# Layer 0 starts its first three projection chunks on rows that carry the scale only, and adds the shift's share as one column per chunk

## The chip, the cores and the metric

The kernel runs on one core of a Trainium2 chip. The metric is the device time of one launch in microseconds (us), as the median of several runs. The engines of the core are named as in the profile: PE is TensorE (PEld its weight loads), DVE is VectorE, ACT is ScalarE, POOL is GpSimd, and SP is the engine whose queue issues the DMAs. L379 is line 379 of the kernel before.

## The reference, cut to what matters

Two decoder layers work on 1024 tokens of width 1024. Each sub-layer computes `x + gate(c) * RMSNorm(f(RMSNorm(x) * (1 + scale(c)) + shift(c)))`. `scale`, `shift` and `gate` are columns of one modulation `silu(c) @ ada_w + ada_b`, the same for all tokens. In layer 0, f starts with one input projection of the modulated rows, `h @ w_in`, whose columns are: a small group (the position part of the keys and the 16 step sizes dt), the latents, 1536 channels xbc, and 1024 channels z. The xbc channels pass through a causal convolution of width 4, a SiLU and the state-space scan.

With a = g * (1 + scale), n the normalised row and s the shift, the row is h = n * a + s, and so h @ w = (n * a) @ w + s @ w. The second term is one number for each output channel, the same for all tokens.

## The kernel before, in words

All rows of the projection's input lie transposed in SBUF (`hT`): two halves of 512 tokens, each with 8 blocks k of 128 of the 1024 inputs, and each block as a pair hi, lo. hi is the value rounded to the type of the matmul, lo is the rest. A chunk is 128 output channels. For one half of a chunk PE runs 24 matmuls of 128x512: for each k hi by hi, hi by lo and lo by hi (L113 to L115, in `mm3`, called from `dense_t`). The weights of a chunk are loaded as one block of 512 KB and split into hi (ACT, L131) and lo (DVE, L132). `chunk` runs both halves and empties the PSUM bank of each (`each`), and then calls `after`.

`first_h` makes `hT` for layer 0. The modulation columns j=1 (scale) and j=0 (shift) are each built from eight 512 KB blocks of `ada_w`: DVE multiplies each by silu(c) and accumulates (L366, L368), and `ada_cols` sums over the partitions on PE (L283, 8 matmuls with a column of ones, recorded as 16). `normal(i)` loads a tile of 128 tokens, ACT takes its sum of squares (L157), POOL makes 1/rms (L150, L151), ACT (i below 4, L350) or DVE (L388) scales the rows, PE transposes 8 blocks (L357) and ACT copies them out (L358) into `xT`. Only when scale and shift are both there, DVE makes v = xT * a + s (L379), ACT writes hi (L143) and DVE or POOL in turn writes lo (L144), for 8 blocks of each half. Tiles 0 to 3 are the first half, tiles 4 to 7 the second.

`mixer0_ssd` then runs the chunks: first three side by side (misc, xbc 0, xbc 1), each first half and then each second half, then xbc 2 to 11 one by one, then z 0 and z 1, then the other z chunks and two latent chunks merged with the state-space scan (`ssd_scan`). `misc` feeds `dt_chain`, a chain of small steps over PE, DVE and ACT (L556 to L579), whose result `csT` goes to DRAM and is read back repeated over the partitions (`csb`, L694, and `esb`, L700). `after` of an xbc chunk is the convolution: four DVE passes over 1024 tokens (L621, L623), a tanh on ACT (L544), one more DVE pass (L545) and the store to DRAM (L549), from where the scan reads it back (L680, L689).

`split_w` and `pump` also push one step of a background job at each weight load: the other modulation columns (`ada_later`, L255, L271, L273).

No order is written out by hand here. A planner lays out the queue of every engine at build time, by the order of the program, by what its own model says is ready and by free buffers. So an engine's order in the trace differs from the order of the source. SP issues all loads and stores of this stage in one queue.

Of the kernel before, what the change touches and what calls it, by code (L numbers as in the profile page):

```python
# [21 lines left out]
P = 128  # L22
T = 1024
NT = T // P
D = 1024
# [21 lines left out]
class Trunk:  # L47
# [292 lines left out]

    def first_h(self, pool, hT):

        nc, I = self.nc, self.I
        xT = self.t(pool, [P, KD, T], "xT")

        def normal(i):
            xt = self.t(pool, [P, D], "xt", bufs=4)
            nc.sync.dma_start(xt, self.x[i])
            if i < 4:
                nc.scalar.activation(xt, xt, AF.Copy, scale=self.rstd(self.sumsq(xt), 1, 1.0 / D))  # L350
            else:
                self.normalise(xt, xt)
            for q in range(2):
                ps = self.bk()
# [3 lines left out]
                nc.scalar.copy(xT[:, 4 * q:4 * q + 4, i * P:(i + 1) * P], ps.rearrange("p (k c) -> p k c", c=P))  # L358

        for j in (1, 0):  # L360
            acc = self.t(pool, [P, 1024], f"acc{j}")
            for i in range(KD):
                w = self.t(pool, [P, 1024], "aw", bufs=5)
                nc.sync.dma_start(w, I["l0_ada_w"][i * P:(i + 1) * P, j * 1024:(j + 1) * 1024])
                if i == 0:
                    nc.vector.tensor_scalar(acc, w, self.cs[:, 0:1], None, op0=ALU.mult)  # L366
                else:
                    nc.vector.scalar_tensor_tensor(acc, w, self.cs[:, i:i + 1], acc, op0=ALU.mult, op1=ALU.add)  # L368
                if i in (1, 4):
                    normal(2 * (1 - j) + i // 4)  # L370
            if j == 1:
                self.setup_gains()
                a = self.ada_scale(0, 1, self.ada_cols(acc), self.gains[0, "mix"])
        self.w0 = self.split_w(self.ring, I["l0_w_in"][0])
        s = self.ada_shift(0, 0, self.ada_cols(acc))
        for h, hs in enumerate(HALVES):
            for k in range(KD):
                v = xT[:, k, hs]
                nc.vector.tensor_scalar(v, v, a[:, k:k + 1], s[:, k:k + 1], op0=ALU.mult, op1=ALU.add)  # L379
                al = slice(0, 512)  # L380
                self.split(self.hk(hT, h, 0, k, al), self.hk(hT, h, 1, k, al), v, nc.gpsimd if k % 2 else nc.vector)
            if h == 0:
                for i in range(4, NT):
                    normal(i)

# [194 lines left out]

    def mixer0_ssd(self, hT, keep):

# [6 lines left out]
        with ExitStack() as e:  # L589
            tmp = self.pool(e, "mix0")  # L590
            sp = self.pool(e, "ssd")
            S["dsk"] = self.t(tmp, [P, 8], "dsk")
# [13 lines left out]
            def misc(h, hs, ps):  # L606
                nc.scalar.copy(mi[0:64, hs], ps[0:64, :])
                nc.vector.tensor_copy(dtT[:, hs], ps[64:80, :])

# [3 lines left out]

            def xbc(j, **kw):
# [11 lines left out]
                return self.chunk("l0_w_in", 6 + j, hT,  # L626
                                  lambda h, hs, ps: nc.scalar.copy(v[:, 3 + h * 512:3 + (h + 1) * 512], ps), after, **kw)

# [22 lines left out]

            self.side_by_side(self.chunk("l0_w_in", 0, hT, misc, misc_end, w=self.w0), xbc(0), xbc(1, bank=self.cx))
            for j in range(2, XBC_N):
                self.side_by_side(xbc(j))

# [1450 lines left out]
    def layer0(self, ew):  # L2106

        self.scratch()
        with ExitStack() as e0:
            self.h_pools(e0, "right")  # L2110
            hT = [self.hT_blocks(4 * h) for h in range(2)]
            with ExitStack() as e:
                self.first_h(self.pool(e, "pre"), hT)
            self.bg = [self.ada_later(0, 2, "gate_m0"), self.ada_later(0, 3, "sf0"), self.ada_later(0, 4, "af0")]
            ek = ExitStack()
            self.mixer0_ssd(hT, self.pool(ek, "keep0"))
            self.mixer0_latent(hT, self.pool(ek, "keepq"))
            self.drain()
# [160 lines left out]
```

## Time and profile before

| what | value |
|---|---|
| median of 3 runs | 3250.03 us (3245.92 to 3252.7) |
| the profiled execution's own time | 3248.5 us |
| its span in the trace | 3246.5 us |
| PE busy in the span | 3038.8 us (94%) |
| DVE, ACT, POOL busy | 2146.6 us (66%), 1310.1 us (40%), 712.9 us (22%) |
| 16 DMA engines, mean | 156 GB/s over the span |
| granted clock of PE, mean | 0.972 |

PE's busy time covers nearly the whole span, so idle stretches of PE are the places where the span can become shorter. The page's picture in 40 slices shows PE at 5 tenths in the first slice (81 us) and at 7 to 9 tenths in slices 3 to 6.

### The profile page before, as it was taken

How to read it: one execution, taken by the hardware profiler on the slowest of the kernel's cores; microseconds unless marked ns; L12 is line 12 of the kernel's file. 1: busy time of each engine (PE TensorE's matmuls, PEld its weight loads, DVE VectorE, ACT ScalarE, POOL GpSimd, SP SyncE). 2: the span in 40 equal slices, each digit the busy share in tenths (PEclk: the TensorE clock that was granted, in tenths of full speed). 3: DMA queues.
4: the chain of work that ended last, by engine and by line, in shares of the span. 5: the costliest groups of instructions: out<-in, count | busy, mean ns of one | idle time of the engine just before them, and what ended most of it. 6: DMA issues, size and time to landing. Idle time of an engine off the chain costs nothing. (4 is left out here: it accounts for less than half of the span.)

```text
span 3246.5 us, 42945 instructions
## 1 busy us (share of the span) xinstructions
PE 3038.8 (94%) x15828; PEld 2462.2 (76%) x15828; DVE 2146.6 (66%) x3371; ACT 1310.1 (40%) x2159; POOL 712.9 (22%) x678
## 2 busy tenths in 40 slices
PE   5987799999999999999899998989999999999998
PEld 4776677777777788787788887777777777888787
DVE  6664366676888778667645546467766788678655
ACT  4343424454542223344533323345655542223443
POOL 3001224310104333001123124012322113322001
PEclk9998889999999999999999999999999999999999
DMA  6555534322655455887324435331211655455854
GB/s 215 138 152 155 145 109 140 101 91 65 225 170 189 156 194 191 288 298 237 116 104 130 137 100 153 89 127 58 80 40 53 237 172 192 156 210 192 293 197 161
DMA packets 246738, 508.00 MB, mean 156 GB/s; under 512 B 27872, under 2 KB 90144, under 8 KB 245504
## 3 DMA queue, kind: packets, MB, share of 16 engines
q1 hardware_dynamic: 246528, 505.26, 47.5%
q8 instruction: 125, 2.05, 0.3%
q14 instruction: 85, 0.70, 0.1%
HBM read 369.04 MB, written 136.13 MB: 156 GB/s over the span
## 5 line engine op out<-in xcount | busy, mean ns | idle before, releaser
L114 PE MATMUL bk<-slab,whi 128*128 128x512 f32 x1208 | 481.8, 399 | 1.9 <-DVE slab L144 1.9
L113 PE MATMUL bk<-slab,whi 128*128 128x512 f32 x784 | 326.0, 416 | 8.2 <-ACT ca L636 4.6
L115 PE MATMUL bk<-slab,wlo 128*128 128x512 f32 x784 | 314.1, 401 | 0.0
L114 PEld LDWEIGHTS bk<-slab,whi 128*128 128x128 f32 x1208 | 232.1, 192 | 53.5 <-issue 2.9
L113 PE MATMUL bk<-T,whi 128*128 128x512 f32 x528 | 210.2, 398 | 1.3 <-DVE blk L1378 1.3
L115 PE MATMUL bk<-T,wlo 128*128 128x512 f32 x528 | 207.9, 394 | 0.0
L113 PEld LDWEIGHTS bk<-slab,whi 128*128 128x128 f32 x784 | 153.1, 195 | 45.3 <-issue 5.4
L150 POOL TENSOR_SCALAR rstd<-ss 128x1 f32<-128x1 f32 (+1 forms) x86 | 32.4, 376 | 688.4 <-ACT junk L157 642.8
L115 PEld LDWEIGHTS bk<-slab,wlo 128*128 128x128 f32 x784 | 152.1, 194 | 33.5 <-issue 0.2
L1174 ACT ACTIVATE whi<-rawa 128x512 fp32r<-128x512 f32 (+1 forms) x108 | 80.6, 750 | 192.5 <-PE bk L114 162.7
L113 PE MATMUL cx<-slab,whi 128*128 128x512 f32 x368 | 146.3, 398 | 6.9 <-ACT blk L1226 5.2
L2095 POOL TENSOR_SCALAR pexp<-pexp,rs 128x640 f32<-128x640 f32 (+7 forms) x128 | 94.4, 741 | 243.8 <-DVE rs L2094 78.9
L114 PE MATMUL cx<-slab,whi 128*128 128x512 f32 x368 | 145.5, 395 | 0.9 <-DVE slab L144 0.9
L115 PE MATMUL cx<-slab,wlo 128*128 128x512 f32 x368 | 145.5, 395 | 0.0
L960 PE MATMUL sm<-ident,pexp 128*128 128x128 f32 x816 | 132.2, 278 | 5.2 <-DVE pexp L950 1.9
L273 DVE SCALAR_TENSOR_TENSOR adaacc<-ada,silu_c,adaacc 128x1024 f32<-128x1024 f32 x70 | 101.7, 1454 | 49.4 <-DMA ada<-in_l_ada_w_dram 49.4
L1402 POOL TENSOR_TENSOR blk<-blk,blk 128x512 f32<-128x512 f32 x22 | 35.3, 1603 | 422.0 <-DVE blk L1398 325.8
L960 PEld LDWEIGHTS sm<-ident,pexp 128*128 128x128 f32 x816 | 93.9, 140 | 40.5 <-issue 18.4
L1175 DVE TENSOR_TENSOR wlo<-rawa,whi 128x512 fp32r<-128x512 f32 (+1 forms) x108 | 118.5, 1097 | 7.4 <-ACT whi L1174 6.7
L113 PEld LDWEIGHTS bk<-T,whi 128*128 128x128 f32 x528 | 99.2, 188 | 26.8 <-DVE blk L1378 1.7
L2091 ACT ACTIVATE pexp<-pexp,nm 128x640 f32<-128x640 f32 (+7 forms) x128 | 94.0, 735 | 62.1 <-DVE nm L2089 49.6
L962 ACT COPY pT<-sm 128x512 f32<-128x512 f32 (+2 forms) x144 | 76.3, 530 | 104.8 <-PE sm L960 104.0
(623 smaller groups left out, 8517.6 us busy)
## 6 DMA issues: line engine op xcount, KB each, us to landing
ada<-in_l_ada_w_dram SPq DMA_DIRECT2D x80, 512.0 KB, 4.2
hid<-blk SPq DMA_DIRECT2D x154, 256.0 KB, 2.0
raw<-in_l_w_in_dram SPq DMA_DIRECT2D x51, 512.0 KB, 4.4
ab<-hid SPq DMA_DIRECT2D x96, 256.0 KB, 3.9
cat<-cat SPq DMA_DIRECT2D x64, 256.0 KB, 2.7
ab<-wt SPq DMA_DIRECT2D x60, 256.0 KB, 4.0
raw<-in_l_w_gate_dram SPq DMA_DIRECT2D x28, 512.0 KB, 3.9
raw<-in_l_w_up_dram SPq DMA_DIRECT2D x28, 512.0 KB, 4.5
```

Source lines behind the costliest of these rows:

```text
L113: mm(out, lh, rh, start=start, stop=False, skip_group_check=more)
L114: mm(out, lh, rl, start=False, stop=False, skip_group_check=more)
L115: mm(out, ll, rh, start=False, stop=stop, skip_group_check=more)
L150: nc.gpsimd.tensor_scalar(r, ss, inv_d, EPS, op0=ALU.mult, op1=ALU.add)
L273: ins = nc.vector.scalar_tensor_tensor(acc, raw, self.cs[:, k:k + 1], acc, op0=ALU.mult, op1=ALU.add)
L960: nc.tensor.transpose(ps[:, k * P:(k + 1) * P], e[:, (b + k) * P:(b + k + 1) * P], self.ident)
L962: (nc.scalar.copy if self.evac else nc.vector.tensor_copy)(pt[:, b:b + m, :], ps[:, :m * P].rearrange("p (k c) -> p k c", c=P))
L1174: nc.scalar.activation(hi, src, AF.Copy)
L1175: (eng or nc.vector).tensor_tensor(lo, src, hi.bitcast(F32), op=ALU.subtract)
L1402: ptt(c, c, state[pm, 0]["u3"], op=ALU.mult)
L2091: nc.scalar.activation(e, e, AF.Exp, bias=nm, scale=-1.0, accum_out=rs)
L2095: nc.gpsimd.tensor_scalar(e, e, rs, 0.0, op0=ALU.mult, op1=ALU.add)
```

## The change: what it does

The order of the first stage becomes: all blocks of the scale column (j=1) and tiles 0 to 3 interleaved; then the first weights; then the scale `a`. `scaled(h)` writes hi and lo of n * a, without the shift (ACT: hi with `a` as scale; DVE: one two-operand instruction for lo). The three first chunks (misc, xbc 0, xbc 1) run on these rows, half by half, into six PSUM banks that stay full. Tiles 4 to 7 are normalised between the first three half-chunks, and the shift column (j=0) is accumulated beside them. When s is there, 24 matmuls of one column (8 for each of the 3 chunks, on the unsplit weights) make s @ w, which is copied to `col`. `misc` and `xbc` add `col` when they empty their banks. Then `shifted(h)` makes the full rows in place: v = xT * a + s, hi on ACT, lo on DVE for three of four blocks and on POOL for the fourth. From xbc 2 on everything works on full rows; xbc 2 and 3 run side by side, and the rest one by one.

Buffers: `xT`, now in two halves, and the three raw weights lie in a pool of their own on the other side of SBUF, closed after the first three chunks' `after`; the scan's pool `sp` is opened behind that. The transposes use the two `sm` banks and no longer the four `bk` banks. The three first weights are split by `split_w` inside `first_h`, which does not push the background job.

```diff
@@ first_h
+        def scaled(h):
             for k in range(KD):
-                v = xT[:, k, hs]
+                v, c = xT[h][:, k, :], a[:, k:k + 1]
+                hi, lo = (self.hk(hT, h, p, k, al) for p in range(2))
+                nc.scalar.activation(hi, v, AF.Copy, scale=c)
+                nc.vector.scalar_tensor_tensor(lo, v, c, hi.bitcast(F32), op0=ALU.mult, op1=ALU.subtract)
+
+        def shifted(h):
+            for k in range(KD):
+                v = xT[h][:, k, :]
                 nc.vector.tensor_scalar(v, v, a[:, k:k + 1], s[:, k:k + 1], op0=ALU.mult, op1=ALU.add)
-                self.split(self.hk(hT, h, 0, k, al), self.hk(hT, h, 1, k, al), v, nc.gpsimd if k % 2 else nc.vector)
+                self.split(self.hk(hT, h, 0, k, al), self.hk(hT, h, 1, k, al), v, nc.gpsimd if k % 4 == 3 else nc.vector)
...
+        for i in range(4):
+            load_a(1, i)
+            load_x(i)
+        load_a(1, 4)
+        self.setup_gains()
+        for i in range(KD):
+            step(1, i)
+            if i + 5 < KD:
+                load_a(1, i + 5)
+            if i % 2:
+                normal(i // 2)
+        for n in range(2):
+            load_w(n)
+        load_x(4)
+        load_x(5)
+        a = self.ada_scale(0, 1, self.ada_cols(acc[1]), self.gains[0, "mix"])
...
+        split_w(0)
+        scaled(0)
+        dense(0, 0)
+        split_w(1)
+        normal(4)
+        normal(5)
+        dense(1, 0)
+        split_w(2)
+        normal(6)
+        normal(7)
+        dense(2, 0)
+        for i in range(KD):
+            step(0, i)
+            if i + 5 < KD:
+                load_a(0, i + 5)
+            if i == 3:
+                scaled(1)
+        dense(0, 1)
+        s = self.ada_shift(0, 0, self.ada_cols(acc[0]))
+        dense(1, 1)
+        ps = self.sm()
+        for n in range(3):
+            for k in range(KD):
+                nc.tensor.matmul(ps[:, n:n + 1], raws[n][:, k * P:(k + 1) * P], s[:, k:k + 1], start=(k == 0),
+                                 stop=(k == KD - 1))
+        col = self.t(self.small, [P, 3], "col", bufs=1)
+        nc.vector.tensor_copy(col, ps[:, :3])
+        dense(2, 1)
+        return banks, col, shifted
@@ mixer0_ssd
+            banks, col, shifted = first
+            three = [(misc, misc_end), xbc(0), xbc(1)]
+            for h, hs in enumerate(HALVES):
+                for (each, _), ps in zip(three, banks):
+                    each(h, hs, ps[h])
+                shifted(h)
+            for _, after in three:
+                after()
+            close_first.close()
+            sp = self.pool(e, "ssd")
+            two = [self.chunk("l0_w_in", 6 + j, hT, *xbc(j)) for j in (2, 3)]
+            self.side_by_side(*two)
```

## Rows read from the trace of the kernel before

**Rows 1.** Busy time of each engine by stretch, from the span's start: the stretch, its length, then PE, PEld, DVE, ACT and POOL busy in us (with their instructions), the granted clock of PE, the share of the DMA engines and what they moved.

```profile
0.00:10.00 10.00, 0.00 (x0) 0.00 (x0) 2.65 (x6) 2.61 (x4) 1.51 (x11) 1.00 0.77 252
10.00:20.00 10.00, 1.97 (x8) 1.57 (x8) 7.71 (x6) 3.40 (x6) 4.74 (x5) 1.00 0.95 341
20.00:30.00 10.00, 5.17 (x24) 5.09 (x24) 3.47 (x5) 4.26 (x6) 2.26 (x2) 1.00 0.92 339
30.00:40.00 10.00, 4.68 (x22) 4.28 (x22) 6.51 (x6) 5.01 (x9) 1.83 (x2) 1.00 0.91 330
...
50.00:60.00 10.00, 6.28 (x28) 5.65 (x29) 8.84 (x9) 6.86 (x12) 7.72 (x7) 1.00 0.18 53
...
27.00:60.00 33.00, 13.42 (x60) 12.30 (x61) 25.67 (x29) 19.69 (x32) 16.73 (x16) 1.00 0.60 215
...
100.00:230.00 130.00, 130.00 (x571) 106.96 (x570) 87.61 (x82) 45.11 (x77) 4.20 (x9) 1.00 0.56 136
```

**Rows 2.** The timeline at the start of the dense work and at the first matmul of chunk xbc 2: start, duration, engine, line, operation.

```profile
60.82 0.78 PE L113 MATMUL bk<-slab,whi 128*128 128x512 f32 x1
...
62.08 0.39 PE L113 MATMUL bk<-slab,whi 128*128 128x512 f32 x1
...
99.69 0.40 PE L113 MATMUL bk<-slab,whi 128*128 128x512 f32 x1
```

**Rows 3.** Who PE waited for between 55 and 300 us: waiting engine, tile and line, whom it waited for; us in total, times, longest.

```profile
PE cx L705 <- DMA bc<-xbc: 14.2, 1, 14.2
PE bk L113 <- ACT ca L636: 4.6, 1, 4.6
```

**Rows 4.** The timeline of ACT with tile 0, 1 and 2 (sum of squares, scaling, copies out).

```profile
8.88 1.06 ACT L157 ACTIVATE junk<-xt 128x1024 bf16<-128x1024 f32 x1 [5.92 <-DMA xt<-in_x_dram]
9.84 0.19 ACT L157 ACTIVATION_READ_ACCUMULATOR junk<-xt 128x1 f32 x1
13.28 1.15 ACT L350 ACTIVATE xt<-xt,rstd 128x1024 f32<-128x1024 f32 x1 [3.25 <-POOL rstd L151]
16.49 0.59 ACT L358 COPY xT<-bk 128x512 f32<-128x512 f32 x1 [0.27 <-PE bk L357]
16.97 1.06 ACT L157 ACTIVATE junk<-xt 128x1024 bf16<-128x1024 f32 x1
25.60 1.06 ACT L157 ACTIVATE junk<-xt 128x1024 bf16<-128x1024 f32 x1 [1.80 <-DMA xt<-in_x_dram]
32.42 0.58 ACT L358 COPY xT<-bk 128x512 f32<-128x512 f32 x1 [0.27 <-PE bk L357]
```

**Rows 5.** The timeline around the two modulation columns: the sums over partitions on PE, and what DVE makes of them.

```profile
22.97 3.41 PE L283 MATMUL sm<-ones,acc 128*128 128x1 f32 x16
26.42 0.17 DVE L294 TENSOR_TENSOR scale<-sm,adab 128x8 f32<-128x8 f32 x1 [7.14 <-PE sm L283]
26.62 0.17 DVE L295 SCALAR_TENSOR_TENSOR scale<-scale,g0mix 128x8 f32<-128x8 f32 x1
```

**Rows 6.** The same sums over partitions in the middle of dense work, from the timeline; and the groups of transposes, L357 in the first 60 us and L960 over the whole span: line, engine, operation, count, busy us, mean ns, idle before.

```profile
2102.49 1.84 PE L283 MATMUL sm<-ones,adaacc 128*128 128x1 f32 x16
...
L357 PE MATMUL bk<-ident,xt 128*128 128x128 f32 x60 | 14.5, 426 | 39.4 <-ACT xt L350 28.2 <-DVE xt L388 11.3
...
L960 PE MATMUL sm<-ident,pexp 128*128 128x128 f32 x816 | 132.2, 278 | 5.2 <-DVE pexp L950 1.9
```

**Rows 7.** Groups of DVE instructions of the first 120 us by shape: count, busy us, mean ns, idle before.

```profile
L368 DVE SCALAR_TENSOR_TENSOR acc<-aw,silu_c,acc 128x1024 f32<-128x1024 f32 x14 | 18.0, 1285 | 5.3 <-DMA aw<-in_l_ada_w_dram 4.9
L379 DVE TENSOR_SCALAR xT<-xT,scale,shift 128x512 f32<-128x512 f32 x16 | 10.8, 723 | 0.1
L144 DVE TENSOR_TENSOR slab<-xT,slab 128x512 fp32r<-128x512 f32 x8 | 8.8, 1095 | 0.2 <-ACT slab L143 0.2
L132 DVE TENSOR_TENSOR wlo<-raw,whi 128x1024 fp32r<-128x1024 f32 x7 | 8.5, 1216 | 0.4 <-ACT whi L131 0.4
L388 DVE TENSOR_SCALAR xt<-xt,rstd 128x1024 f32<-128x1024 f32 x4 | 5.0, 1261 | 1.2 <-POOL rstd L151 1.2
L608 DVE COPY ca<-bk 16x512 f32<-16x512 f32 x2 | 1.4, 682 | 0.0
```

**Rows 8.** Groups of ACT instructions of the first 120 us, in the same form.

```profile
L143 ACT ACTIVATE slab<-xT 128x512 fp32r<-128x512 f32 x16 | 9.2, 624 | 6.4 <-DVE xT L379 6.4
L131 ACT ACTIVATE whi<-raw 128x1024 fp32r<-128x1024 f32 x7 | 7.4, 1057 | 7.3 <-PE bk L114 4.1 <-PE cx L114 3.3
```

**Rows 9.** The timeline of POOL and DVE between 49 and 57 us.

```profile
49.76 5.21 POOL L144 TENSOR_TENSOR slab<-xT,slab 128x512 fp32r<-128x512 f32 x3
...
49.75 0.67 DVE L144 TENSOR_TENSOR slab<-xT,slab 128x512 fp32r<-128x512 f32 x1
50.35 1.77 DVE L388 TENSOR_SCALAR xt<-xt,rstd 128x1024 f32<-128x1024 f32 x1
52.05 1.78 DVE L144 TENSOR_TENSOR slab<-xT,slab 128x512 fp32r<-128x512 f32 x1
56.62 0.75 DVE L388 TENSOR_SCALAR xt<-xt,rstd 128x1024 f32<-128x1024 f32 x1 [0.44 <-POOL rstd L151]
```

**Rows 10.** What ACT waited for over the first 400 us, and the landing times of the read that it waited for, from issue to landing.

```profile
ACT elast L724 <- DMA csb<-csT: 94.1, 14, 10.8
...
DMA to landing us min/median/max: 8.9/10.7/14.9
```

More of the change, by code (lines that the diff above doesn't have):

```diff
@@ L339, in hk, with first_h, load_x, load_a @@
         return hT[half][part][k // 4][:, k % 4, cols]
-    def first_h(self, pool, hT):
+    def first_h(self, pool, keep, hT):
         nc, I = self.nc, self.I
-        xT = self.t(pool, [P, KD, T], "xT")
+        xT = [self.t(keep, [P, KD, 512], f"xT{h}") for h in range(2)]
+        al = slice(0, 512)
+        x, aw = {}, {}
+        def load_x(i):
+            x[i] = self.t(pool, [P, D], "xt", bufs=4)
+            nc.sync.dma_start(x[i], self.x[i])
+        def load_a(j, i):
+            aw[j, i] = self.t(pool, [P, 1024], "aw", bufs=5)
+            nc.sync.dma_start(aw[j, i], I["l0_ada_w"][i * P:(i + 1) * P, j * 1024:(j + 1) * 1024])
         def normal(i):
-            xt = self.t(pool, [P, D], "xt", bufs=4)
-            nc.sync.dma_start(xt, self.x[i])
+            xt = x.pop(i)
             if i < 4:
@@ L357, in normal @@
                     nc.tensor.transpose(ps[:, k * P:(k + 1) * P], xt[:, kk * P:(kk + 1) * P], self.ident)
[L358 to L373, printed above, removed]
@@ new lines, in first_h, with step, load_w @@
+        acc = [self.t(pool, [P, 1024], f"acc{j}") for j in range(2)]
+        def step(j, i):
+            if i == 0:
+                nc.vector.tensor_scalar(acc[j], aw.pop((j, i)), self.cs[:, 0:1], None, op0=ALU.mult)
+            else:
+                nc.vector.scalar_tensor_tensor(acc[j], aw.pop((j, i)), self.cs[:, i:i + 1], acc[j], op0=ALU.mult,
+                                               op1=ALU.add)
+        raws, w = [], []
+        def load_w(n):
+            raws.append(self.t(keep, [P, 1024], f"first{n}"))
+            nc.sync.dma_start(raws[n], I["l0_w_in"][(0, 6, 7)[n]])
@@ new lines, in shifted, with dense @@
+        def shifted(h):
+            for k in range(KD):
+                v = xT[h][:, k, :]
+                nc.vector.tensor_scalar(v, v, a[:, k:k + 1], s[:, k:k + 1], op0=ALU.mult, op1=ALU.add)
+                self.split(self.hk(hT, h, 0, k, al), self.hk(hT, h, 1, k, al), v, nc.gpsimd if k % 4 == 3 else nc.vector)
+        banks = [[self.bk(), self.bk()], [self.bk(), self.bk()], [self.cx(), self.cx()]]
+        def dense(n, h):
+            for _ in self.dense_t(w[n], hT, h, banks[n][h]):
+                pass
@@ new lines, in first_h @@
+        load_x(7)
+        for i in range(5):
+            load_a(0, i)
+        split_w(0)
[17 more added lines that the diff above has]
+        s = self.ada_shift(0, 0, self.ada_cols(acc[0]))
@@ L579, in dt_chain, with mixer0_ssd @@
         nc.sync.dma_start(S["csT"], csT)
-    def mixer0_ssd(self, hT, keep):
+    def mixer0_ssd(self, hT, keep, first, close_first):
         nc, I, S = self.nc, self.I, self.S
@@ L590, in mixer0_ssd @@
             tmp = self.pool(e, "mix0")
-            sp = self.pool(e, "ssd")
             S["dsk"] = self.t(tmp, [P, 8], "dsk")
@@ L606, in misc @@
             def misc(h, hs, ps):
-                nc.scalar.copy(mi[0:64, hs], ps[0:64, :])
-                nc.vector.tensor_copy(dtT[:, hs], ps[64:80, :])
+                nc.scalar.activation(mi[0:64, hs], ps[0:64, :], AF.Identity, bias=col[0:64, 0:1])
+                nc.vector.tensor_scalar(dtT[:, hs], ps[64:80, :], col[64:80, 0:1], None, op0=ALU.add)
             def misc_end():
@@ L612, in misc_end, with xbc @@
                 self.dt_chain(tmp, tmp, dtT)
-            def xbc(j, **kw):
+            def xbc(j):
                 v = self.t(tmp, [P, T + 3], "cv", bufs=4)
@@ L625, in after, with each @@
                     self.to_cat(S["xbc"], j, a)
-                return self.chunk("l0_w_in", 6 + j, hT,
-                                  lambda h, hs, ps: nc.scalar.copy(v[:, 3 + h * 512:3 + (h + 1) * 512], ps), after, **kw)
+                def each(h, hs, ps):
+                    o = v[:, 3 + h * 512:3 + (h + 1) * 512]
+                    if j < 2:
+                        nc.scalar.activation(o, ps, AF.Identity, bias=col[:, j + 1:j + 2])
+                    else:
+                        nc.scalar.copy(o, ps)
+                return each, after
             def z(j):
@@ L650, in latent @@
                 S["rkv"] = self.rstd(self.token_sumsq(sq, self.sm()), NT, 1.0 / 256)
-            self.side_by_side(self.chunk("l0_w_in", 0, hT, misc, misc_end, w=self.w0), xbc(0), xbc(1, bank=self.cx))
-            for j in range(2, XBC_N):
-                self.side_by_side(xbc(j))
+            banks, col, shifted = first
[10 more added lines that the diff above has]
+            self.side_by_side(*two)
+            for j in range(4, XBC_N):
+                self.side_by_side(self.chunk("l0_w_in", 6 + j, hT, *xbc(j)))
             for j in range(2):
@@ L2112, in layer0 @@
             with ExitStack() as e:
-                self.first_h(self.pool(e, "pre"), hT)
+                ex = ExitStack()
+                first = self.first_h(self.pool(e, "pre"), self.pool(ex, "xT", side="right"), hT)
             self.bg = [self.ada_later(0, 2, "gate_m0"), self.ada_later(0, 3, "sf0"), self.ada_later(0, 4, "af0")]
             ek = ExitStack()
-            self.mixer0_ssd(hT, self.pool(ek, "keep0"))
+            self.mixer0_ssd(hT, self.pool(ek, "keep0"), first, ex)
             self.mixer0_latent(hT, self.pool(ek, "keepq"))
```

17 lines of the change are left out of this document (9 added, 8 removed).

## The prediction

> **What bounds the kernel now.** I read the busy shares first: PE is busy for 94% of the span, so time is to be found where PE stands still. I then cut the start into stretches [rows 1]. Up to 60 us PE has hardly any work, and the DMA engines are at 0.77 to 0.95 of their time for the first 30 us and at 0.18 by 50 to 60 us: the stage begins as a load and ends as a chain over ACT, POOL and DVE. The timeline shows the first dense matmul at 60.82 us and the first of chunk xbc 2 at 99.69 [rows 2]. From 100 to 230 us PE is busy without a gap, 571 matmuls in 130.0 us, 0.228 us each [rows 1]. The list of PE's waits shows two later stops, 14.2 and 4.6 us, at the hand-over from the convolutions to the scan [rows 3]. They follow the last xbc chunk by a chain that the change does not touch. So PE sets the end from 60.8 us on, and what comes before is a wait in front of it. The matmuls of the first three chunks are worth bringing forward into that wait; I ask what they then cost and what is late next.
>
> **The start of the dense work.** Before, it needs scale, shift and the first four tiles; after, scale and four tiles.
> - Earliest: a 512 KB block is 0.524 MB. The scale's eight blocks and four tiles are 12 blocks, 6.29 MB; the first 20 us move 2.52 + 3.41 = 5.93 MB and the rest goes at 339 GB/s [rows 1], so the last block is there at 21.1. One accumulation of 1.28 [rows 7], the sum over partitions and the two small instructions (22.97 to 26.79, 3.8) [rows 5], hi 0.62 [rows 8] and lo 0.68 (half of the 1.285 of the same instruction on 1024) [rows 7]: 27.5 us.
> - Latest: the tiles go one after the other as now. Tile 0 takes from 8.88 to 17.08, the next ones about 7 each (16.97 to 23.8, 25.60 to 33.0) [rows 4]: 17.1 + 21 + 1.3 = 39.4 us.
> - I take ACT packed, since all four tiles are loaded early: tile 0 to 17.08, then 3 x 3.58 of ACT work (1.06 + 0.19 + 1.15 + 2 x 0.59) [rows 4], 1.06 for the first weights' hi [rows 8], then 0.62 + 0.68: 30.2 us.
>
> **What PE does until xbc 2.** Six half-chunks are 144 matmuls, 144 x 0.228 = 32.8 us in both kernels. Before, 60.82 to 99.69 is 38.87, so the dt chain (and the slow first matmuls, 1.26 for three in [rows 2]) costs 6.1; it stays, now behind. New on PE's path, since PE no longer waits there:
> - 32 transposes of tiles 4 to 7: 132.2 / 816 = 0.162 each in busy stretches, 14.5 / 60 = 0.242 in the start [rows 6]: 5.2 or 7.7; I take 5.2, as they stand between dense matmuls.
> - the sum over partitions of the shift: 1.84 inside dense work, 3.41 outside [rows 5, 6]; 1.8.
> - 24 one-column matmuls. None is in the trace in this place, but the sum over partitions has the same form, 8 of them in 1.84 to 3.41 [rows 5, 6]: 5.5 to 10.2; I take 5.5, the row inside dense work.
>
> Sum: 30.2 + 32.8 + 6.1 + 5.2 + 1.8 + 5.5 = 81.6, against 99.7: 18.1 us earlier.
>
> **What is late next.** The blocks of the shift are the 20th to 27th: by 40 us 2.52 + 3.41 + 3.39 + 3.30 = 12.6 MB, 24 blocks, were moved [rows 1], so they end near 45, before PE asks for their sum (about 60). They are hidden. `shifted(0)` overwrites rows that the third half-chunk has read by about 54 and can run beside the fifth and the column matmuls; `shifted(1)` must wait for the sixth and has the two first halves of xbc 2 and 3 as cover, 48 x 0.228 = 10.9 us. ACT's hi are 8 x 0.62 = 5.0. DVE is the tight one. From 27 us until the second half is whole it has: 16 new lo (10.9), 5 weight lo at 1.22 (6.1), 4 normalisations (0.75 to 1.26 each), the shift's accumulation (0.75 + 7 x 1.28 = 9.7), 16 L379 at 0.5 to 0.72, 12 lo at 0.67 to 1.10, two bank copies (1.4) [rows 7, 9]: 47 us alone, 58 by the group means. PE gives it from 27 to about 92, 65 us. So it fits at 0.73 to 0.89 of its time; between 27 and 60 DVE reached 25.67 / 33 = 0.78 [rows 1]. Some stalls must come of it: at the least they cost 0, at the worst 14 (B, below). I take 4.5, which also covers the turn of two `sm` banks between transposes and copies where four `bk` banks served. It lies nearer the lower end because the means hold collisions with POOL that become fewer: POOL makes 4 lo and not 8.
>
> That collision is in the trace: while POOL worked 5.21 us on three lo, a normalisation on DVE took 1.77 where it takes 0.75 alone, and a lo 1.78 for 0.67 [rows 9]. [...]
>
> Two more edits I cost at nothing. The background job is pushed two times fewer until the scan; its steps move to the drain behind the latents, where PE has other work; without that cover each is a load and a pass of 1.28. The PSUM banks stay full until `col`, and xbc 2 needs two of them 5.4 us (24 x 0.228) after that, against copies of about 0.6; if the copies queue behind the hi of `shifted(0)` on ACT, up to 5.0 is lost, inside the 14.
>
> From xbc 2 on everything moves as it stands: DVE has 130 - 87.6 = 42 us free until 230 [rows 1] to work off the later convolutions, and the two stops behind it [rows 3] follow the last chunk by the same chain. So 18.1 - 4.5 = 13.6 us. The profiled execution took 3248.5, 2.0 more than its span and 1.5 less than the median: 3248.5 - 13.6 = 3234.9 in its terms, 3236 for the median.
>
> **The rivals.**
> - A, the late start: the planner lays the four tiles out one after the other as now [rows 4], and dense work starts at 39.4. For it: tiles 2 and 3 ran like that. Against it: their loads were issued late, and now they come early. 9.2 us less: gain 4.4 to 8.9, depending on whether DVE then still stalls PE; 3244.
> - B, DVE becomes the bound of the start: it needs the 58 us at the 0.78 that it reached, 74 us, from 27 to 101, where PE wants the last block near 92 (30.2 + 32.8 + 5.2 + 1.8 + 5.5 + 10.9 + 5.4). It stands 9, and 5 more for ACT's queue; gain 18.1 - 14 = 4; 3246. For it: the sum of rows 7; against it: less work for POOL.
> - C, slower: the scan is laid out worse. Its order is made anew by the planner once the stage before it moves, and its pool opens later. ACT's queue stops there for repeated reads of `csT`, 14 times for 94.1 us, each landing 10.7 us after its issue [rows 10]. Two more such stops on the scan's path cost 21.4 and turn the gain: 3248.5 - 13.6 + 21.4 + 1.5, 3258. It decides from the second stop on. For it: PE is not full in the scan; against it: the scan's instructions and their order in the program are unchanged.
> - D: the first chunks run early and PE waits anyway at the hand-over, because the last convolution ends no earlier. DVE's 42 us of slack speak against it; no gain, 3250.
>
> **How the numbers follow.** Forecast 0.62, its own range 3228 (start 27.5, no stall) to 3241 (stalls of 9). A 0.15, B 0.08, C 0.10, D 0.05. A measurement of this kernel tells about 0.2%, 6.5 us, from no change. Faster by more: nearly all of the forecast and most of A, 0.74. Within: the rest of A, most of B and D, 0.14. Slower: C and a little of B, 0.12. The range goes from 3223 (start 27.5, no stall, and some of the dt chain's waits filled) to 3251, which takes in A, B and D.
>
> **What would show it.** The first dense matmul at 28 to 33 us (A: 38 or later); the first of xbc 2 at 80 to 90 where it was at 99.69; 48 records of the one-column matmuls in 5 to 7 us; DVE's lo at 0.7; PE full from there to the hand-over; and the last xbc chunk earlier by the same amount as the end. The prediction is wrong if the start is early but the first xbc 2 matmul is not (B), or if xbc 2 is early and the end is not (C, D).

## The result and the profile after

The changed kernel is slower: 3268.8 us (median of 4 runs, 3267.75 to 3270.73) against 3248.0 beside it (4 runs, 3245.46 to 3252.7); ratio 1.0061, 95% interval 1.0046 to 1.0076. The forecast was 3236 with a range of 3223 to 3251: outside, and on the other side. The profiled execution took 3270.7 us with a span of 3269.0. PE is busy 3055.1 us, DVE 2158.7, ACT 1319.4, POOL 702.1; the mean granted clock is 0.965.

Where the start of some work stands in the two traces, in us from the span's start:

| | before | after | after minus before |
|---|---|---|---|
| first dense matmul | 60.82 | 29.98 | -30.8 |
| first matmul of xbc 2 | 99.69 | 82.79 | -16.9 |
| tanh of xbc 8, the ninth convolution | 183.04 | 180.58 | -2.5 |
| hand-over: first B x C matmul of the scan | 253.94 | 246.78 | -7.2 |
| last store of the scan's result y | 460.4 | 462.4 | +2.0 |
| first V copied out of PSUM, behind the drain of the background job | 507.2 | 533.7 | +26.5 |
| end of the span | 3246.5 | 3269.0 | +22.5 |

So the start does what it should, the lead is gone by the end of the scan, and within 75 us behind that the kernel loses 24.5 us, a little more than the whole of the result. The timeline of PE after (start, duration, engine, line, operation; in brackets the idle time before it and what ended that):

```profile
29.98 0.79 PE L113 MATMUL bk<-slab,whi 128*128 128x512 f32 x1 [1.27 <-ACT slab L396]
68.04 7.21 PE L455 MATMUL sm<-shift,first 128*128 128x1 f32 x48
82.79 0.50 PE L113 MATMUL bk<-slab,whi 128*128 128x512 f32 x1
89.61 0.79 PE L115 MATMUL bk<-slab,wlo 128*128 128x512 f32 x1 [3.97 <-DVE wlo L132]
246.78 1.22 PE L797 MATMUL cx<-bc 128*128 128x128 f32 x4 [9.59 <-DMA bc<-xbc]
527.35 3.57 PE L283 MATMUL sm<-ones,adaacc 128*128 128x1 f32 x16 [22.10 <-DVE adaacc L273]
```

The timeline of PE before, at the last two of these places:

```profile
253.94 1.22 PE L705 MATMUL cx<-bc 128*128 128x128 f32 x4 [14.22 <-DMA bc<-xbc]
499.39 3.57 PE L283 MATMUL sm<-ones,adaacc 128*128 128x1 f32 x16
```

The first and the third line of after answer to [rows 2], the last to the sum of [rows 6] at another place: the background job's last sum over partitions (of `af0`). It waits 22.1 us for DVE, and the V matmuls stand behind it. The list of waits from 400 to 560 us shows the same (waiting engine, tile, line, whom it waited for; total, times, longest), after:

```profile
PE sm L283 <- DVE adaacc L273: 22.1, 1, 22.1
```

and before, where no wait of PE for that line of DVE is listed and PE's longest is

```profile
PE sm L804 <- DVE esb L765: 3.1, 1, 3.1
```

What DVE waited for is in the queue of SP. The loads of the modulation's blocks (L255) behind the scan, after:

```profile
479.25 20.54 SPq L255 DMA_DIRECT2D ada<-in_l_ada_w_dram  x4
509.96 0.33 SPq L255 DMA_DIRECT2D ada<-in_l_ada_w_dram  x1
515.58 0.33 SPq L255 DMA_DIRECT2D ada<-in_l_ada_w_dram  x1
522.05 0.38 SPq L255 DMA_DIRECT2D ada<-in_l_ada_w_dram  x1
```

and before:

```profile
436.11 13.90 SPq L255 DMA_DIRECT2D ada<-in_l_ada_w_dram  x2
462.54 0.33 SPq L255 DMA_DIRECT2D ada<-in_l_ada_w_dram  x1
468.33 24.16 SPq L255 DMA_DIRECT2D ada<-in_l_ada_w_dram  x4
```

Both have seven loads there, each behind the pass of the one before it, because `ada` has one buffer; the last three after are 5.6 and 6.5 us apart. Before, the first is issued at 436.1, while the scan still runs, and the seven fit under its end: DVE's last pass is at 498.05 with 1.29 us, and PE's sum begins at 499.39. After, the first is issued at 479.3, 43 us later, and the last pass ends at 527.3. DVE's last pass before, from its timeline:

```profile
498.05 1.29 DVE L273 SCALAR_TENSOR_TENSOR adaacc<-ada,silu_c,adaacc 128x1024 f32<-128x1024 f32 x1
```

The 43 us come from the column ahead of it (`sf0`). `adaacc` has one buffer too, so the last column can start only when PE has summed the one before. That sum runs within the scan before, and behind it after. From the timelines of PE, before and then after:

```profile
424.72 1.95 PE L283 MATMUL sm<-ones,adaacc 128*128 128x1 f32 x16 [1.45 <-DVE esb L765]
```

```profile
473.57 1.84 PE L283 MATMUL sm<-ones,adaacc 128*128 128x1 f32 x16
```

The windows of the stretch behind it (as in [rows 1]), after and then before, show PE busy for less of the time and its granted clock lower, 0.66 against 0.88:

```profile
500.00:550.00 50.00, 27.90 (x123) 24.08 (x123) 23.36 (x32) 13.07 (x23) 16.65 (x18) 0.66 0.51 161
```

```profile
500.00:550.00 50.00, 45.56 (x170) 33.43 (x171) 26.77 (x44) 21.70 (x38) 25.07 (x33) 0.88 0.46 146
```

### The profile page after: what moved, and what is told of

The parts are those of the page before. It is cut to its first block, busy times and chain, and to the rows that moved or that the text cites. A ratio compares the mean times of both kernels' runs of the same rounds, so it can differ in the third digit from the quotient of the medians.

```text
span 3269.0 us, 43076 instructions
## 1 busy us (share of the span) xinstructions
PE 3055.1 (93%) x15876; PEld 2471.9 (76%) x15876; DVE 2158.7 (66%) x3392; ACT 1319.4 (40%) x2175; POOL 702.1 (21%) x674
## 5 line engine op out<-in xcount | busy, mean ns | idle before, releaser
L114 PEld LDWEIGHTS bk<-slab,whi 128*128 128x128 f32 x1208 | 234.7, 194 | 56.1 <-issue 3.1
```

Of the source, the lines that this page charges most:

```text
L114: mm(out, lh, rl, start=False, stop=False, skip_group_check=more)
```

## The experiments

All ratios are to the kernel before, run on the same chip in turn, with 95% intervals. The runs used several chips, and before's own median was 3239 to 3248 us, so ratios are compared and not times. One profile's hand-over can differ by a few us without a trace in the time (e7 and e8 below), so a claim here rests on a ratio or on more than one trace.

### The drain: two pushes

Theory: the two pushes of the background job that the change leaves out (its first weights don't go through the pushing `split_w`) move its last steps behind the scan, and PE waits there. First they are put back into the changed kernel (e1), then taken out of the kernel before (e2).

```diff
@@ e1: changed kernel, mixer0_ssd
             banks, col, shifted = first
+            self.pump()
+            self.pump()
@@ e2: kernel before, split_w
-        self.pump()
+        self.nw += 1
+        if self.nw > 3:
+            self.pump()
```

> The changed kernel with two pushes of the background job put back, just before the first three chunks' banks are emptied; nothing else differs. Theory 1 (the change made two pushes fewer, so the end of the second background column and two more blocks of the third fall into the drain behind the latents, whose loads run one at a time, and PE stands 22.1 us on their sum in front of the V matmuls): that wait falls under 2 us, the last background block lands near 500 us and not 527, and the time is 3268.8 - 22, about 3247, or 3238 if the 9 us lost in the scan stage also came from background loads in SP's queue. Rival (the planner laid out the stage behind the scan worse for other reasons, and the background job only happens to be last): the wait turns up elsewhere between 450 and 560 us and the time stays at 3260 or more.

> The kernel before, with the pushes of the background job left out at the weight loads of xbc 0 and xbc 1 and nothing else changed. Theory 1: the kernel before loses by it what the changed kernel loses at the drain, 20 to 30 us: about 3248 + 25 = 3273, with PE's wait on adaacc in front of the V matmuls at 20 us or more and the start (first dense matmul at 60.8) untouched. Rival (layout): within 5 us of before.

e1: ratio 1.0001 (0.9991 to 1.0012), 0.0060 below the changed kernel; no such wait, the sum of `sf0` back at 424.9, V at 505.0. e2: 1.0073 (1.0058 to 1.0088), with the sum of `sf0` at 472.1, V at 530.0, the hand-over at 249.6, and this line in its timeline of PE:

```profile
523.59 3.58 PE L286 MATMUL sm<-ones,adaacc 128*128 128x1 f32 x16 [21.55 <-DVE adaacc L276]
```

Two pushes fewer cost the kernel before about as much as the changed kernel lost. This explains the sign. It leaves a second question: with the drain mended the first xbc 2 matmul is at 83.43, 16 us early, and the time is that of before.

### What else the start pays: weights and columns

In e1 PE waits 6.4 us for the low part of the weights of xbc 2, whose split stands behind the rows with shift in DVE's queue. e4 splits these weights ahead of them. e5 is e1 with the 24 one-column matmuls spread over the matmuls of the fifth half-chunk; e12 is e4 without them, so its first three chunks lack the shift's share.

```diff
@@ e4: e1, mixer0_ssd
+            early = [self.split_w(self.ring, I["l0_w_in"][6 + j]) for j in (2, 3)]
...
-            two = [self.chunk("l0_w_in", 6 + j, hT, *xbc(j)) for j in (2, 3)]
+            two = [self.chunk("l0_w_in", 6 + j, hT, *xbc(j), w=early[j - 2]) for j in (2, 3)]
@@ e5: e1, first_h: three behind each k of dense(1, 1)
+            for n, k in cols[3 * kk:3 * kk + 3]:
@@ e12: e4, first_h
-        nc.vector.tensor_copy(col, ps[:, :3])
+        nc.vector.tensor_copy(col, s[:, 0:3])
```

> The changed kernel with the two pushes put back, and the weights of xbc 2 and 3 loaded and split before the banks of the first three chunks are emptied in the order of the program. Theory: PE's wait of 4.0 us on wlo at 89.6 us and the slow matmuls behind it (PE at half its clock from 90 to 94 us) come from DVE taking that lo behind the shifted rows; both go, and the hand-over to the scan comes 5 to 7 us earlier than in e1, the time 4 to 7 us under e1. Rival (DVE is full there, so the split only pushes the shifted rows back): PE waits for slab in place of wlo, and the time is within 2 us of e1.

> The changed kernel with the two pushes put back, and the 24 one-column matmuls laid between the dense matmuls of the fifth half-chunk, three behind each block k, and not in one piece behind it. Theory (PE's clock falls to its lower level in the 7.2 us of one-column matmuls and the dense matmuls behind start at that level): the granted clock between 68 and 78 us stays at 1.00, the columns cost 5.5 us and not 7.2 + about 2.5 behind, and the first matmul of xbc 2 comes about 4 us earlier than in e1. Rival (these matmuls cost the same wherever they are): within 1 us of e1.

> The kernel of e4 without the 24 one-column matmuls; the three columns are copied from the first three of the shift, so the share of the shift in the first three chunks is left out. This gives the price of the columns. PE gets 7.2 us back, and 2 to 3 more if the lower clock at 74 to 80 us goes with them: the first matmul of xbc 2 at 73 to 76 where it is at 83.0 in e4. The clock at 74 to 80 us stays at 1.00 if the one-column matmuls are what lowers it. At the hand-over: if DVE's queue (whose wait of 6 to 7 us for the columns goes too) or PE sets it, 5 to 9 us earlier than 250.5, ratio 0.996 to 0.997; if the loop of csb reads sets it alone, within 2 us.

e4: 0.9986 (0.9973 to 0.9999), hand-over 250.5 where e1 has 255.8; the wait is gone, and the ratio is 0.0015 below that of e1, with intervals that overlap. e5: 1.0015 (0.9998 to 1.0031), xbc 2 at 89.98, so 6.6 us worse than e1; its expectation fell. e12: 0.9971 (0.9959 to 0.9983), xbc 2 at 74.57 where e4 has it at 83.00, hand-over 241.5, 9.0 us earlier than e4. The columns cost 8.4 us of PE where I had 5.5. The windows of four us from 66 to 82 us show the granted clock there, first after, then e12 (PE, PEld, DVE, ACT, POOL busy, then the granted clock):

```profile
66.00:70.00 4.00, 4.00 (x29) 3.64 (x27) 2.13 (x3) 1.49 (x3) 1.31 (x1) 1.00 0.00 0
70.00:74.00 4.00, 4.00 (x26) 4.00 (x27) 0.00 (x0) 0.00 (x0) 0.00 (x0) 0.67 0.00 0
74.00:78.00 4.00, 4.00 (x13) 3.42 (x14) 2.65 (x6) 2.52 (x5) 0.00 (x0) 0.50 0.00 0
78.00:82.00 4.00, 4.00 (x19) 3.15 (x17) 3.93 (x8) 3.27 (x7) 1.29 (x1) 0.98 0.30 66
```

```profile
66.00:70.00 4.00, 4.00 (x19) 3.31 (x18) 3.24 (x7) 2.50 (x4) 0.00 (x0) 1.00 0.69 239
70.00:74.00 4.00, 4.00 (x19) 3.20 (x18) 4.00 (x4) 1.44 (x4) 1.91 (x1) 1.00 0.45 141
74.00:78.00 4.00, 4.00 (x21) 3.15 (x20) 3.97 (x8) 3.63 (x6) 0.00 (x0) 1.00 0.34 122
78.00:82.00 4.00, 4.00 (x21) 3.09 (x20) 3.97 (x7) 2.28 (x5) 1.27 (x1) 1.00 0.00 0
```

and one window of e5:

```profile
62.00:86.00 24.00, 24.00 (x84) 20.94 (x84) 10.66 (x21) 7.52 (x14) 1.96 (x2) 0.51 0.01 3
```

PE counts as busy in all of these, and yet its granted clock goes down: after has 0.67 from 70 to 74 us, within the row of one-column matmuls, and 0.50 from 74 to 78; from 78 to 82 us, behind dense matmuls, it is back at 0.98. In e12, without the row, it stays at 1.00 in these windows. In e5, where the one-column matmuls are mixed into dense work, it is 0.51 over 24 us. The first of these 24 us are not the columns' alone: from 62 to 66 us, behind the sum over partitions, after has 0.68, e12 0.58 and e5 0.56.

### Is the earlier PE slack?

First theory: from 100 us on DVE's convolutions set the pace, and PE's lead is worth nothing. e6 and e13 are e4 with 40 more matmuls (e13 writes them into the bank of xbc 2, so that they stand ahead of it); e7 and e8 take work out of the way of the first convolution.

```diff
@@ e6: e4, mixer0_ssd; e13 has the same loop in chunk, into out[h] of xbc 2
+            for i in range(40):
+                nc.tensor.matmul(dummy, early[0][0][:, 0:P], self.hk(hT, 0, 0, 7, slice(0, 512)), start=(i == 0),
+                                 stop=(i == 39))
@@ e7: e4, first_h: the additions leave shifted(h)
         s = self.ada_shift(0, 0, self.ada_cols(acc[0]))
+        added(0)
+        added(1)
@@ e8: e7, mixer0_ssd
-                shifted(h)
+                if h == 0:
+                    shifted(h)
+            misc_end()
+            shifted(1)
```

> The kernel of e4 with 40 matmuls of 128x512 on rows of the first half, into a bank that nobody reads, ahead of the first matmul of xbc 2 (40 x 0.228 = 9.1 us of PE). Theory (from 100 us on the convolutions on DVE set the pace, so an earlier xbc 2 is worth nothing at the hand-over to the scan): xbc 2 starts 9 us later than in e4, and the first B x C matmul, 250.5 in e4, moves by less than 2.5 us; the ratio to before stays within 0.001 of that of e4 (0.9986). Rival (PE sets the hand-over, and what e4 has over before is simply its earlier PE): the hand-over moves to 257 to 260, ratio 1.001 to 1.002.

> In e6 the 40 matmuls stood at 104 to 113 us, in the middle of xbc 2, and held up ACT's queue there; the hand-over came 3.7 us later than in e4. Here they write into the bank of xbc 2's first half and stand right ahead of it, at 83 us. Theory (from 100 us on the convolutions on DVE and the csb loop set the pace; PE's lead is slack): xbc 2 starts 9 us later than in e4 (92), the hand-over within 2.5 us of 250.5, the ratio within 0.001 of e4's. Rival (PE's lead is worth its full length): hand-over at 258 to 261, ratio 0.0022 to 0.003 above that of e4.

> The kernel of e4 with the 16 in-place additions of the shift for both halves written directly behind the shift, ahead of the one-column matmuls, so that DVE makes them in the 7 us in which it waits for the columns in e4. Theory (DVE's queue behind the shift sets when the convolutions begin, 105 us in e4, and they the hand-over): the 8 additions of the second half, about 4.5 us, leave DVE's queue, the first convolution starts 3 to 5 us earlier and the hand-over comes 3 to 5 us earlier than 250.5; ratio to before about 0.997. Rival (the hand-over hangs on something else): the first convolution starts earlier and the hand-over stays within 1.5 us.

> The kernel of e7 with the dt chain written ahead of the rows with shift of the second half, so that DVE and ACT work on it before those. Theory (the dt chain stands behind the rows with shift in the queues): csT is stored 3 to 8 us earlier than in e7; xbc 2's second half may wait for its rows by as much; the first convolution stands behind both and starts at the same time as in e7, so the hand-over moves by less than 2 us. Rival (the dt chain alone holds the convolutions back): convolutions and hand-over come 3 us or more earlier than in e7.

e6: the 40 did not stand ahead of xbc 2 but at 104 to 113 us, so it doesn't test what it was meant to; 1.0008 (0.9997 to 1.0019), hand-over 254.2. e13: xbc 2 at 96.63, 13.6 us later than in e4 (the 40 took 10.8, partly at a lower granted clock, 0.60 from 86 to 90 us, behind a wait of 1.9); hand-over 257.05, 6.6 later; 1.0022 (1.0010 to 1.0034), 0.0036 or 11.7 us above e4. The theory fell: PE's lead is not all slack, though of the 13.6 us only 6.6 arrive at the hand-over. e7: the first convolution starts 1.3 us earlier than e4's 105.45, and not 3 to 5; 0.9990 (0.9979 to 1.0002), hand-over 254.8. e8: it starts at 100.68 and the hand-over is at 248.8, 6 us before that of e7, where under 2 was expected; yet the time is the same, 0.9990 (0.9981 to 0.9999). So the order on DVE within the start isn't it either.

One number stood out over these traces: from the tanh of xbc 8 to the hand-over it takes 70.9 us before, 70.6 in e4, 70.3 in e13, 70.4 in e12 and 70.4 in e8, whatever came ahead (66.2 in after, 69.3 to 72.9 in e1, e6 and e7). The timeline of ACT before, in that stretch:

```profile
183.04 1.06 ACT L544 ACTIVATE ca<-ca 128x1024 f32<-128x1024 f32 x1 [0.86 <-DVE ca L623]
197.58 0.22 ACT L724 ACTIVATE elast<-csb 128x8 f32<-128x8 f32 x1 [8.62 <-DMA csb<-csT]
198.17 1.06 ACT L544 ACTIVATE ca<-ca 128x1024 f32<-128x1024 f32 x1
214.89 0.22 ACT L724 ACTIVATE elast<-csb 128x8 f32<-128x8 f32 x1 [10.81 <-DMA csb<-csT]
220.00 1.06 ACT L544 ACTIVATE ca<-ca 128x1024 f32<-128x1024 f32 x1 [4.21 <-DVE ca L623]
235.10 0.22 ACT L724 ACTIVATE elast<-csb 128x8 f32<-128x8 f32 x1 [9.18 <-DMA csb<-csT]
235.22 1.04 ACT L544 ACTIVATE ca<-ca 128x1024 f32<-128x1024 f32 x1
```

The planner has put the scan's repeated reads of `csT` among the last convolutions. The tanh of the next chunk stands in ACT's queue behind an instruction that waits for such a read, and the next read is issued when ACT has used up one of the two buffers (at 186.47 us, where its eight L718 end at 186.44). So a loop of read, ACT and tanh goes round at 15 to 22 us a chunk. The tanh at 198.17 and at 235.22 start right behind an `elast` that waited 8.62 and 9.18 us. The tanh at 220.00 waits for DVE, whose queue is held by the same read, from its timeline before:

```profile
214.89 0.17 DVE L723 TENSOR_TENSOR dec<-csb,cs 128x8 f32<-128x8 f32 x1 [7.70 <-DMA csb<-csT]
```

This loop is long, but it carries a lead over and does not use it up. e4 is 3.2 us ahead of before at the tanh of xbc 8 and 3.4 at the hand-over, e12 11.9 and 12.4. By its expectation, e12's hand-over should have moved by at most 2 us against e4 if the loop alone set it; it moved by 9.0. So the rest of the lead is lost ahead of the tanh of xbc 8.

### The loop of csb reads

e9 gives csb four buffers in e4, e10 in the kernel before, e11 in e8. e14 (on e4) and e15 (on the kernel before) take the reads out of the convolutions: the last part of the dt chain, which makes and stores csT, moves behind the last convolution. e16 and e17 are these two with four buffers.

```diff
@@ e9, e10, e11: ssd_prep
-            csb = self.t(pool, [P, 8, P], "csb", bufs=2)
+            csb = self.t(pool, [P, 8, P], "csb", bufs=4)
@@ e14, e15: the end of dt_chain, from the csT tile on, becomes cs_out; in after() of xbc
                     self.to_cat(S["xbc"], j, a)
+                    if j == XBC_N - 1:
+                        self.cs_out(tmp)
```

> The kernel of e4 with four buffers in place of two for the repeated reads of csT (csb). In before and in e4 ACT waits five times for such a read between 182 and 252 us, 7.6 to 11.6 us each, with the tanh of the last convolutions queued behind it. Theory (from 186 us on this loop of read, ACT and tanh sets the pace, 16 to 20 us a chunk where DVE alone takes 8.3): with reads under way two further ahead some of these waits go, and the hand-over comes 8 us or more earlier than 250.5; ratio to before 0.994 to 0.997. Rival (PE or DVE set the pace there too): the waits go and the hand-over stays within 2 us; ratio 0.9986.

> The kernel before with four buffers in place of two for csb, and nothing of the change. In e9 this edit, put on e4, gave a ratio of 0.9948 and took the scan from 204 us (250.5 to 454.5) to 184. Theory (the gain of e9 is the scan's, and has nothing to do with the change): before gains the same 12 us or so here, ratio 0.9955 to 0.997, the scan from 253.9 to 460.4 gets 15 to 20 us shorter. Rival (the buffers fit the scan only with the change's order): ratio above 0.999.

> The kernel of e8 (two pushes early, weights of xbc 2 and 3 early, in-place additions ahead of the columns, dt chain ahead of the second half's rows) with four csb buffers. If the parts add up, the ratio is that of e9 within 0.001, 0.9945 to 0.9955; the change then adds 0 to 4 us of gain to what e10 has alone.

> The kernel of e4 with the last part of the dt chain (transposes of cs, csT, its store), and with it the repeated reads csb, moved behind the last convolution, where csT takes the buffer that the second-to-last tanh frees. ACT then no longer waits for csb between 180 and 250 us. Theory (the loop of csb reads, standing in ACT's queue among the last convolutions, takes back the lead of PE): tanh of xbc 9 to 11 follow at 8 to 11 us as those before them do; xbc 11 is stored near 210 where e4 has 236.9, and the hand-over to the scan comes at 220 to 230 where e4 has 250.5. The scan's first block then waits about 15 us for its csb; ratio 0.993 to 0.997. Rival (DVE or PE set the pace there in any case): the hand-over stays within 5 us of 250.5.

> The same edit on the kernel before. PE is full from 99.69 us on, and xbc 2 to 11 take 10 x 10.9 us, so xbc 11 ends near 209 there; with conv, tanh, store and the read back of bc the hand-over comes at 232 to 240 where before has 253.9. If the loop of csb reads was what hid the change's earlier PE, the hand-over of e14 is 10 to 16 us ahead of this one, and its ratio 0.003 to 0.005 lower. Rival (DVE's queue hides it too): e14 is less than 5 us ahead, ratios within 0.0015.

> The kernel of e14 with four csb buffers. If both parts add up (approach to the scan from e14, the scan's own waits from e9), the ratio is 0.002 to 0.004 below that of e14 and below e9's 0.9948: 0.989 to 0.993.

> The kernel of e15 with four csb buffers, nothing of the change. Between e16 and this one stands what the change (with its two pushes and weights early) is worth once the loop of csb reads is out of the way: 10 to 16 us, 0.003 to 0.005 of ratio, by the theory; under 0.0015 by the rival.

| | ratio (interval) | xbc 2 | tanh of xbc 8 | hand-over | last y store |
|---|---|---|---|---|---|
| e4 | 0.9986 (0.9973 to 0.9999) | 83.00 | 179.9 | 250.5 | 454.5 |
| e9, e4 with four buffers | 0.9948 (0.9933 to 0.9962) | 83.88 | 190.6 | 258.6 | 442.9 |
| e10, before with four buffers | 0.9955 (0.9942 to 0.9969) | 98.26 | 187.3 | 256.3 | 438.4 |
| e11, e8 with four buffers | 0.9957 (0.9940 to 0.9974) | | 191.0 | 261.4 | 443.7 |
| e14, e4 with late csb | 0.9978 (0.9966 to 0.9990) | 83.98 | 171.2 | 225.0 | 454.3 |
| e15, before with late csb | 1.0017 (1.0008 to 1.0026) | 94.56 | 180.2 | 233.8 | 464.4 |
| e16, e14 with four buffers | 0.9969 (0.9957 to 0.9981) | | 170.7 | 223.4 | 445.0 |
| e17, e15 with four buffers | 1.0016 (1.0008 to 1.0025) | | 181.2 | 234.7 | 459.4 |

e9's ratio came as expected and its reason did not: the hand-over got later by 8 us, and the gain is the scan's, which takes 184 us and not 204. The stretch from the tanh of xbc 8 to the hand-over stays at 68.0, 69.0 and 70.4 us in e9, e10 and e11, so it is not the number of buffers that makes it long. e10 has a scan of 182 us, where before has 206, without any of the change. e9, e10 and e11 can't be told apart: all beat the kernel before by some 14 to 17 us (0.0043 to 0.0052), and the change adds nothing that can be measured to four buffers.

e14 and e15 show whether the lead passes without the reads. The hand-over, from their timelines of PE, e14 and then e15:

```profile
225.01 1.22 PE L806 MATMUL cx<-bc 128*128 128x128 f32 x4 [3.85 <-DMA bc<-xbc]
```

```profile
233.81 0.71 PE L711 MATMUL cx<-bc 128*128 128x128 f32 x4 [2.16 <-DMA bc<-xbc]
```

PE's wait there, 14.2 us before, is down to 2 to 4. In e15 the tanh now follows PE at the 10.9 us of a chunk, with 0.86 us of waiting, from its timeline of ACT:

```profile
158.46 1.06 ACT L544 ACTIVATE ca<-ca 128x1024 f32<-128x1024 f32 x1 [0.86 <-DVE ca L627]
169.34 1.06 ACT L544 ACTIVATE ca<-ca 128x1024 f32<-128x1024 f32 x1 [0.86 <-DVE ca L627]
180.22 1.06 ACT L544 ACTIVATE ca<-ca 128x1024 f32<-128x1024 f32 x1 [0.86 <-DVE ca L627]
```

And the lead passes: 10.6 us at xbc 2, 9.0 at the tanh of xbc 8, 8.8 at the hand-over, and 0.0039 of ratio, 12.6 us, in the time; for e16 against e17 it is 0.0047, 15.2 us. So the change (with its two pushes and early weights) is worth about the 13.6 us that I had forecast (each ratio is known to 0.001, so the difference to some 5 us), from a lead at xbc 2 of 10.6 us and not of 18.1, and only where the csb reads and the end of the dt chain don't stand among the convolutions. Taking them away is no gain for itself: e15 is slower than before, since the scan then waits for the reads that it had prefetched (DVE's `dec` waits 61.7 us for csb in it, where before has 38.0, and it is 230 us from the hand-over to the last store, where before has 206). Two expectations were missed in the time: e14 was to reach 0.993 to 0.997, and e16 0.989 to 0.993, so the gains of the late reads and of the four buffers don't add up.

### Where the lead is lost

The convolutions do not start earlier. The first pass of the first one, from the timelines of DVE, before and then after:

```profile
100.43 0.79 DVE L621 TENSOR_SCALAR ca<-cv,cw,cb 128x1024 f32<-128x1024 f32 x1
```

```profile
100.11 0.79 DVE L696 TENSOR_SCALAR ca<-cv,cw,cb 128x1024 f32<-128x1024 f32 x1
```

PE is 16.9 us ahead at xbc 2, but DVE has the rows with shift in its queue until 88.0 us and then, among other work, the dt chain, and waits only 2.1 us between 76 and 100 us. The first pass of the first and of the third convolution in the pairs of kernels:

| | xbc 2 on PE | first convolution | third | tanh of xbc 8 | hand-over |
|---|---|---|---|---|---|
| before | 99.69 | 100.43 | 128.13 | 183.04 | 253.94 |
| after | 82.79 | 100.11 | 123.92 | 180.58 | 246.78 |
| e4 | 83.00 | 105.45 | 132.38 | 179.89 | 250.50 |
| e14 | 83.98 | 95.42 | 112.36 | 171.24 | 225.01 |
| e15 | 94.56 | 94.79 | 111.19 | 180.22 | 233.81 |

The csb reads take their share behind that. In e4's timeline of ACT the very first tanh stands behind the first csb read:

```profile
117.32 1.28 ACT L819 ACT_TABLE_LOAD   x1 [8.09 <-DMA csb<-csT]
118.62 0.22 ACT L819 ACTIVATE elast<-csb 128x8 f32<-128x8 f32 x1
118.74 1.05 ACT L620 ACTIVATE ca<-ca 128x1024 f32<-128x1024 f32 x1
```

In e14 the same tanh runs at 102.8; in the kernel before, where the planner put it ahead of the read, at 108.6. At the third convolution e14 is 20 us ahead of e4: 10 before the first convolution, which in e4 stands behind the whole dt chain, and 10 between the first and the third, where DVE waits 9.4 us in e4 (csb, the stores of the convolutions, the weights) and not at all in e14. Behind that DVE is faster than PE, with a tanh every 5.8 to 9.3 us in e4 where PE takes 10.9 a chunk, so a lead comes back chunk by chunk. In e14 it is there by xbc 8, in e4 only 3.2 us of it.

Open: e14 and e15 take away the first reads, the last reads and the end of the dt chain in one edit, and no run separated them. Nor did I follow why after, alone, loses 9 us within the scan (7.2 ahead at the hand-over, 2.0 behind at the last store).

## Why the prediction was wrong, point by point

**The start was right in its numbers, in part by luck.** Dense work begins at 29.98 (forecast 30.2, packed on ACT), and A is refuted. But ACT is not what set it: ACT has done the tiles and the first weights at 26.9 and waits 2.31 us for the scale, whose sum over partitions runs from 25.1 to 28.7. I had that path at 27.5. xbc 2 starts at 82.79 (forecast 81.6), where two misses cancel. The dt chain, 6.1 in the sum, has only 0.6 us on PE ahead of xbc 2. The 144 dense matmuls take 39.9 us where I had 32.8, since some run at 0.43 us and not 0.228, at the start (31.6 to 33.7 us) and where the granted clock is lower (0.68 from 62 to 66 us, 0.50 from 74 to 78). Of the other terms, the transposes took 1.03 to 1.14 us a tile, 4.3 in all, where I had 5.2; the sum over partitions 2.1 for 1.8; the columns 7.2 for 5.5. In e4 they took 6.6 and by e12 cost 8.4, with the granted clock at 0.50 behind them from 74 to 78 us where e12 has 1.00; a lower clock was not in the sum. The 16 new lo took 0.67 each (two groups of eight in 5.38 and 5.39 us), the undisturbed price: POOL had no work beside them, so these rows do not show what the new lo take beside POOL's work.

**The stall was of the right size.** I took 4.5 us; PE waits 4.0 for the weights' lo behind the rows with shift.

**The step that failed: "Two more edits I cost at nothing. The background job is pushed two times fewer until the scan; its steps move to the drain behind the latents, where PE has other work".** It cost 24.5 us. PE has no other work there: the sum of the last column stands ahead of V in PE's order, the loads are serial through one buffer, and the column before it holds `adaacc` until its own sum. The trace of before could have told it: the last pass ends at 499.34 and the sum begins at 499.39, so this chain had no slack. I named the cover and the price of a step without it (a load and a pass), but did not look whether the cover was there. The price was too low as well: at the 5.6 and 6.5 us between loads, two steps make an estimated 12 us, and the two pushes moved the sum of `sf0` by 49 us and V by 26.5.

**The second step that failed: "From xbc 2 on everything moves as it stands".** I took PE for the pace up to the hand-over, because it is busy without a gap from 100 to 230 us. But the convolutions do not move with it: their first pass on DVE is at 100.11 for 100.43, and of the 16.9 us at xbc 2 the tanh of xbc 8 has 2.5 left. In after PE then stands still for 9.1 of the 130 us. That is rival D, at 0.05; its time, no gain, is what e1 measured. I rejected it by DVE's 42 us of slack, a sum over a stretch in which DVE's queue is full at the start and waits later: before, from 60 to 256 us, ACT waits 45.2 us for csb reads and DVE's `dec` 13.7. [Rows 10] had such waits and their landing times. I put them under C, as a price of a new order, and did not ask which convolutions stood behind them already. My sum for DVE ended with the rows and put nothing for the dt chain behind them. e14 and e15 show that the end of the dt chain and the reads together hold the lead back; how much falls to each is open.

**The sum.** Forecast -13.6 us, measured +22.2 between the profiled executions. The rows after account for it: -7.2 at the hand-over, +9.2 over the scan, +24.5 over the drain, and 4 us less from there to the end. C has the right sign, but its mechanism, two more stops for csb, is not what made it.

## What to carry to other kernels

Where a change shifts the steps of a background job, follow the job to its last step and read whether the work behind it starts at once; if it does, there is no cover, and look which buffer the job's last part needs and who frees it: here two steps cost 24.5 us. A busy engine is not the pace of a stage if its end is handed on by another queue: look where the next engine's first instruction moves, and through that stage for the waits of every engine on DMAs, also of one that is mostly idle. And a lead that vanishes is tested by taking the suspected loop out of both versions and comparing the pair: here 0.0039 and 0.0047 of ratio appeared where e4 had shown 0.0014.

## What the runs showed of the hardware that I had not expected

- PE's granted clock fell in stretches in which the profile calls PE busy throughout: to 0.50 from 74 to 78 us, behind 48 records of one-column matmuls in 7.2 us, where e12, without them, has 1.00; and to 0.51 over 24 us in e5, where they stand between dense matmuls. Spreading them out made it worse (6.6 us).
- A ring of four buffers instead of two for a read that lands 9 to 15 us after its issue [rows 10] took 20 us off a scan of 204 us (e9) and 24 off one of 206 (e10), and 14 to 17 us off the time.
